# Mixture of experts: a second branch per expert behind the first product, and the gather and combine placed between the products

## The chip, the cores and the metric

The kernel runs on one core of one Trainium2 chip. The metric is device time in microseconds of the core, the median of three runs. One execution is also taken by the hardware profiler; its span is shown in the profile.

## The reference

The whole model is one dense block pair (a hybrid mixer and a SwiGLU, twice), and then a second block with two kinds of attention and a mixture of experts. The change touches only the mixture of experts, for 256 tokens of width 1024, 32 experts, four of them for each token:

```python
def clamped_swiglu(hdn):
    x_glu = jnp.minimum(hdn[..., :D_EXPERT], 7.0)
    x_lin = jnp.clip(hdn[..., D_EXPERT:], -7.0, 7.0)
    return x_glu * jax.nn.sigmoid(1.702 * x_glu) * (x_lin + 1)

logits = xt @ w_router + b_router
top_v, top_i = lax.top_k(logits, 4)
gates = jax.nn.softmax(top_v, axis=-1)
# for each expert e, over the tokens that chose it:
y = clamped_swiglu(x_e @ w_gate_up[e] + b_gate_up[e]) @ w_down[e] + b_down[e]
# out[token] += gate * y
x = x + gt_f * rms_norm(out, g_post_ffn)
```

`w_gate_up[e]` is 1024 x 2048 and `w_down[e]` 1024 x 1024, in float32: 12 MiB of weights for each expert, 384 MiB in all, each read once.

## The kernel before

The dense part takes the first 830 us or so and is not touched. The expert loop starts at line 1421 and is written out for 32 experts. A framework takes the program as written, tracks which instruction reads or writes which tile, and orders the instructions of each engine by readiness and by their place in the program; an instruction block under `tc.If` is placed as one unit on the engines that take part.

*Weights.* An expert's weights are 12 tiles of 1 MiB: eight of `w_gate_up` (`ws`, 128 rows each), four of `w_down` (`wd`). They go through a ring of 18 buffers (`RING2`, `etile`, line 1150). Only SyncE (SP) issues these loads, in order. At the head of expert e the loop asks for six tiles of expert e+1 (`nw.load(NEXT)`, line 1430), behind the branch of expert e for the other six (`nw.rest()`, line 1477). Tile i of the ring can be loaded when the 18th tile before it has been read for the last time.

*One expert.* Each expert has 64 places for tokens in the usual case. `g1` (line 1208) is the first product: 64 rows by 2048 columns over eight chunks of the depth, eight matmul instructions each in the trace, 64 in all, two column groups of the array at a time. The first two chunks and the bias (`begin`, line 1378) are asked for at the end of the expert before. `act` (line 1222) is the clamped SwiGLU: VectorE (DVE), ScalarE (ACT), DVE three times. `g2` (line 1234) turns the result with four transposes, copies it (line 1241), and makes the second product in 32 matmul instructions; ACT and DVE then split the result in a high and a low part (`yh`, `yl`, lines 1249 and 1250).

*A pair of experts.* Two experts share one gather and one combine. In an odd expert `pick_up` (line 1368) gathers the tokens of the next two with 32 one-hot matmuls, `places` turns the one-hot matrices for the combine (line 1257), `slot_gates` (line 1267) picks the gates. In an even expert `combine` (line 1286) adds the pair before to `acc`: eight matmuls (line 1284), in four PSUM banks, and four additions on DVE (line 1292). In expert 16 the bias of the second product is added for all experts. In the text "even" and "odd" are the number of the expert, counted from 0.

*The branch.* An expert with more than 64 tokens needs further places. `tc.If(n > 64)` at line 1463 stands behind `g2`; inside it `further(64)` gathers 32 more tokens (`extra_xt`), multiplies them with the same `ws` (`extra_in`) and `wd` (`extra_out`), and a nested `tc.If(n > 96)` (line 1470) does so again. PE, ACT and DVE take part. The number `n` is read into registers of the three engines (line 1436) from a one-element tile that POOL copies (line 1435). With these inputs experts 1 and 14 enter the outer branch, none the inner one. `many()` (line 1386) has one more branch, after expert 29, for over 128 tokens; it isn't entered.

*PSUM.* In this loop there are four banks for the first product (tag `g1`) and four for all the rest (`ps`).

*Residual.* `h`, 256 x 1024 in SBUF, holds the residual rows until the last additions (line 1490).

Of the kernel before, what the change touches and what calls it, by code (L numbers as in the profile page):

```python
# [20 lines left out]
P = 128  # L21
# [11 lines left out]

RING2 = (-1, 0, 1, -1, 2, 3, 4, 5, 6, 7, -1, -1, 8, 9, 10, 11, 12, 13)
EARLY = 10

MANY = 30

NEXT = len(RING2) - KC - KC // 2

# [58 lines left out]
def kernel_body(ctx, tc, I, out, stop=None, dbg=None):  # L99
# [20 lines left out]
    def wtile():  # L120
        return ring.tile([P, 2048], F32, tag="w", name=nm("w"))
# [4 lines left out]

    h = cpool.tile([P, 2, D], F32, name="h")
    nc.sync.dma_start(h[:, 0, :], I["x"][0:P, :])
# [659 lines left out]
    with ExitStack() as cx:  # L788
# [361 lines left out]
        def etile():  # L1150
            i = RING2[turn[0] % len(RING2)]
            turn[0] += 1
            if i < 0:
                return wtile()
            return (ring2 if i < 8 else ring3).tile([P, 2048], F32, tag=f"w{i}", name=nm("w2"))

        class Expert:

            def __init__(self, up, down, split=False):
                self.up, self.down, self.ws, self.wd, self.split = up, down, [], [], split  # L1160

            def load(self, n):
                for _ in range(n):
                    r = etile()
                    if len(self.ws) < KC:
                        nc.sync.dma_start(r, self.up(len(self.ws)))
                        self.ws.append(r)
                    else:
                        k = len(self.wd)
                        if self.split and k == KC // 2 - 1:  # L1170
                            for i in range(2):
                                nc.sync.dma_start(r[:, i * D:(i + 1) * D], self.down(k).rearrange("(p k) f -> p k f", k=2)[:, i])
                        else:
                            nc.sync.dma_start(r.rearrange("p (k f) -> p k f", k=2), self.down(k).rearrange("(p k) f -> p k f", k=2))
                        self.wd.append(r)
# [14 lines left out]
    with ExitStack() as cx:  # L1190

        mo = cx.enter_context(tc.tile_pool(name="mo", bufs=2, reuse_waits="tile"))

        bb = mo.tile([P, 2, 512], F32R, name="bb", bufs=1)
# [13 lines left out]
        def g1(banks, xt, ws, kcs):  # L1208

            for kc in kcs:  # L1210
                for b in range(2):
                    for a in range(2):
                        c0 = b * D + a * 512
                        TE.matmul(banks[b][64 * a:64 * a + 64, :], lhsT=xt[:, kc, :], rhs=ws[kc][:, c0:c0 + 512], start=kc == 0, stop=kc == KC - 1)  # L1214
# [100 lines left out]
        def extra_in(a, xt, sel, ws):  # L1315

            banks = [ps()[:, :256] for _ in range(2)]
            for b in range(2):
                for i in range(4):
                    TE.matmul(banks[b][32 * i:32 * i + 32, :], lhsT=sel(i // 2).to_broadcast([P, 32]),  # L1320
                              rhs=bb[:, b, 256 * (i % 2):256 * (i % 2) + 256].bitcast(F32), start=True, stop=False)
            for kc in range(KC):
                for b in range(2):
                    for i in range(4):
                        c0 = b * D + 256 * i
                        TE.matmul(banks[b][32 * i:32 * i + 32, :], lhsT=xt[:, kc, :], rhs=ws[kc][:, c0:c0 + 256], start=False, stop=kc == KC - 1)
            act(a[:, :256], banks)

# [11 lines left out]
        def extra_out(a, slot0, pm, gt, wd):  # L1340
            a, pg = a[:, :256], a[:, 256:].rearrange("p (a b) -> p a b", a=2)
            for t in range(2):
# [18 lines left out]
        def gathered(banks):  # L1361

            xt = mo.tile([P, KC, P], F32, tag="xt", name=nm("xt"), bufs=1)
            for i, q in enumerate(banks):
                (V.tensor_copy if i % 2 else S.copy)(xt[:, 4 * i:4 * i + 4, :].rearrange("p a b -> p (a b)"), q)
            return xt
# [19 lines left out]
        def many():  # L1386
# [4 lines left out]
            with tc.If(most > P):  # L1391
# [3 lines left out]
                with tc.For_i(0, NE, 1) as ei:  # L1395
# [3 lines left out]
                    for c in range(4):  # L1399
                        a1 = mo2.tile([P, 512], F32, tag="g", name=nm("og"), bufs=1)  # L1400
                        extra_in(a1, extra_xt(32 * c, lambda t: now[:, t, 0:1]), lambda q: now[:, 4 + q, 0:1], w.ws)
                        extra_out(a1, 32 * c, lambda t: now[:, t, 0:1], lambda t: now[:, 2 + t, 0:1], w.wd)
# [10 lines left out]
        nxt = begin(0, first)  # L1413
        ahead = places(), slot_gates(0)
        for t in range(2):
            S.copy(xmh[:, t, :], xm[:, t, :])
            V.tensor_sub(xml[:, t, :], xm[:, t, :], xmh[:, t, :].bitcast(F32))
        acc = xpool.tile([P, 2, D], F32, tag="xh", name="acc")
        G.memset(acc, 0.0)
        y = last = None  # L1420
        for e in range(NE):
# [14 lines left out]
            n = nc.values_load(ne[0:1, 0:1], engines=[mybir.EngineType.PE, mybir.EngineType.Activation, mybir.EngineType.DVE],  # L1436
                               min_val=0, max_val=T)
            if e + 1 == NE:
                gp2 = mo.tile([P, D], F32, tag="xt", name="gp2", bufs=1)
                nc.scalar.dma_start(gp2, lastd[0].partition_broadcast(P))  # L1440
            elif j:
                xt = pick_up()
                ahead = places(), slot_gates(e + 1)
            if j == 0:
                if last is not None:
                    combine(*last)
                if e == NE // 2:

                    g4, bd = [mo.tile([P, 2, 512], F32, tag=tag, name=nm(tag), bufs=1) for tag in ("yh", "yl")]
                    g4, bd = g4[:, :, :P], bd[:, 0, :256]  # L1450
                    gT = mo2.tile([P, T], F32, tag="oT", name="gT", bufs=1)
                    nc.scalar.dma_start(bd, I["b_down"])
                    for t in range(2):
                        G.tensor_copy(g4[:, t, :].rearrange("p (a b) -> p a b", a=4), copies4(gate[:, t, :]))
                    turned(gT, g4)
                    combine4(gT, bd)
                y = [mo.tile([P, 2, 512], F32R, tag=tag, name=nm(tag), bufs=1) for tag in ("yh", "yl")]
            if e + 1 == NE:
                fin = [[psum.tile([P, 512], F32, tag="g1", name=nm("fin")) for _ in range(2)] for _ in range(2)]
                carry(fin)  # L1460
            g2(a, w.wd, y, j)
            pm, gt = (lambda t: posm[:, t, e:e + 1]), (lambda t: gate[:, t, e:e + 1])
            with tc.If(n > 64):  # L1463
                def further(slot0):
                    o = mo2.tile([P, 512], F32, tag="g", name=nm("og"), bufs=1)
                    extra_in(o, extra_xt(slot0, pm), lambda q: qe[:, q, e:e + 1], w.ws)
                    extra_out(o, slot0, pm, gt, w.wd)

                further(64)
                with tc.If(n > 96):  # L1470
                    further(96)
                if e + 1 == NE:
                    carry(fin, True)
            if e + 1 == MANY:
                many()
            if e + 1 < NE:
                nw.rest()
                nxt = begin(e + 1, nw)
# [9 lines left out]
        for t in range(2):  # L1488
            for a, b, o in zip(halves(acc[:, t, :]), halves(h[:, t, :]), halves(out[t * P:(t + 1) * P, :])):
                V.scalar_tensor_tensor(b, a, r[t][:, 0:1], b, ALU.mult, ALU.add)  # L1490
                nc.sync.dma_start(o, b)
# [42 lines left out]
```

## Time and profile before

| | |
|---|---|
| median of three runs | 1964.48 us (1957.91 to 1967.62) |
| the profiled execution | 1965.33 us, its span 1963.6 us |
| PE busy | 1774.7 us, 90% of the span |
| DVE, ACT, POOL busy | 783.2, 522.4, 164.5 us |
| DMA | 568.48 MB, mean 290 GB/s |
| mean granted clock of PE | 0.957 |

PE is the matmul engine, PEld its weight loads, which overlap with matmuls. A name with a q (PEq, PEldq, SPq) is the engine's sequencer, where waits, branches and the issue of DMAs stand; these do not count as busy time. Ends of matmuls are modelled. L1463 is line 1463 of the kernel before. Times in a timeline are microseconds from the start of the span.

### The profile page before, as it was taken

How to read it: one execution, taken by the hardware profiler on the slowest of the kernel's cores; microseconds unless marked ns; L12 is line 12 of the kernel's file. 1: busy time of each engine (PE TensorE's matmuls, PEld its weight loads, DVE VectorE, ACT ScalarE, POOL GpSimd, SP SyncE). 2: the span in 40 equal slices, each digit the busy share in tenths (PEclk: the TensorE clock that was granted, in tenths of full speed). 3: DMA queues.
4: the chain of work that ended last, by engine and by line, in shares of the span. 5: the costliest groups of instructions: out<-in, count | busy, mean ns of one | idle time of the engine just before them, and what ended most of it. 6: DMA issues, size and time to landing. Idle time of an engine off the chain costs nothing. (4 is left out here: it accounts for less than half of the span.)

```text
span 1963.6 us, 23687 instructions
## 1 busy us (share of the span) xinstructions
PE 1774.7 (90%) x9432; PEld 1083.8 (55%) x9432; DVE 783.2 (40%) x1267; ACT 522.4 (27%) x892; POOL 164.5 (8%) x261
## 2 busy tenths in 40 slices
PE   8999999999999999988888898988888989898986
PEld 6888997787899788734333332334333333233322
DVE  5677775667777667522112112211212111211122
ACT  5645444565444455311000101010001010101011
POOL 1131210113111130010000000000000000000000
PEclk9999999999999999888999999999899999999998
DMA  9537786433788673816999899996789999999976
GB/s 303 147 118 236 246 278 228 152 129 114 249 260 277 211 257 129 352 50 249 398 372 379 358 413 379 379 380 252 287 348 373 378 417 383 380 378 407 393 289 254
DMA packets 160403, 568.48 MB, mean 290 GB/s; under 512 B 15426, under 2 KB 66124, under 8 KB 111060
## 3 DMA queue, kind: packets, MB, share of 16 engines
q1 hardware_dynamic: 149560, 552.42, 72.9%
q10 hardware_dynamic: 9852, 11.57, 1.8%
q0 software_dynamic: 800, 1.77, 0.8%
q8 instruction: 141, 2.31, 0.5%
q14 instruction: 50, 0.41, 0.1%
HBM read 563.06 MB, written 2.66 MB: 288 GB/s over the span
## 5 line engine op out<-in xcount | busy, mean ns | idle before, releaser
L1214 PE MATMUL g<-w,xt 128*64 128x512 f32 x2048 | 518.6, 609 | 31.5 <-PEq L1463 17.6
L1214 PEld LDWEIGHTS g<-w,xt 128*64 128x64 f32 x2048 | 147.5, 138 | 303.8 <-issue 292.3
L251 DVE TENSOR_TENSOR wlo<-w,whi 128x1024 fp32r<-128x1024 f32 x203 | 256.4, 1268 | 100.7 <-ACT whi L250 96.7
L1247 PE MATMUL ps<-w,aT 128*64 128x512 f32 x1024 | 264.1, 674 | 22.6 <-ACT aT L1241 22.6
L250 ACT CAST whi<-w 128x1024 fp32r<-128x1024 f32 x203 | 211.2, 1045 | 180.0 <-PE ps L257 87.2
L256 PE MATMUL ps<-xh,whi 128*128 128x256 f32 x792 | 227.9, 288 | 0.0
L257 PE MATMUL ps<-xh,wlo 128*128 128x256 f32 x792 | 223.3, 282 | 0.0
L258 PE MATMUL ps<-xl,whi 128*128 128x256 f32 x792 | 223.2, 282 | 0.0
L1247 PEld LDWEIGHTS ps<-w,aT 128*64 128x64 f32 x1024 | 80.2, 155 | 186.7 <-issue 155.0
L1250 DVE TENSOR_TENSOR yl<-ps,yh 64x512 fp32r<-64x512 f32 x64 | 44.1, 689 | 339.4 <-ACT yh L1249 338.4
L256 PEld LDWEIGHTS ps<-xh,whi 128*128 128x128 f32 x792 | 149.5, 189 | 2.1 <-PE ps L405 1.0
L257 PEld LDWEIGHTS ps<-xh,wlo 128*128 128x128 f32 x792 | 149.4, 189 | 2.1 <-issue 1.7
L258 PEld LDWEIGHTS ps<-xl,whi 128*128 128x128 f32 x792 | 149.4, 189 | 0.0
L1226 ACT ACTIVATE g<-g 128x512 f32<-128x512 f32 x32 | 19.2, 601 | 347.8 <-DVE g L1225 347.8
L1249 ACT CAST yh<-ps 64x512 fp32r<-64x512 f32 x64 | 37.1, 579 | 267.4 <-PE ps L1247 266.6
L1111 DVE TENSOR_SCALAR pos<-idio,posm 128x64 fp32r<-128x64 f32 x64 | 12.9, 251 | 221.7 <-PE ps L1267 221.6
L1225 DVE TENSOR_SCALAR g<-g 128x512 f32<-128x512 f32 x32 | 22.1, 692 | 181.3 <-PE g L1214 181.3
L1239 PE MATMUL ps<-idio,g 128*128 128x128 f32 x128 | 26.6, 339 | 71.1 <-DVE g L1232 71.1
L1218 POOL CAST pick<-qe 128x128 fp32r<-128x128 f32 x32 | 9.4, 293 | 953.9 <-PE g L1220 953.6
L256 PE MATMUL ps<-whi,xh 128*128 128x512 f32 x176 | 72.5, 412 | 2.1 <-ACT xh L214 1.3
L1258 ACT CAST pT<-ps 128x256 fp32r<-128x256 f32 x16 | 6.0, 372 | 254.4 <-PE ps L1257 247.9
L1239 PEld LDWEIGHTS ps<-idio,g 128*128 128x128 f32 x128 | 19.3, 211 | 96.7 <-issue 50.9
(372 smaller groups left out, 2527.3 us busy)
## 6 DMA issues: line engine op xcount, KB each, us to landing
w<-in_w_gate_up_dram SPq DMA_DIRECT2D x256, 1024.0 KB, 18.0
w<-in_w_down_dram SPq DMA_DIRECT2D x149, 1024.0 KB, 10.6
w<-in_w_in_dram SPq DMA_DIRECT2D x32, 1024.0 KB, 6.8
w<-in_w_ada_dram SPq DMA_DIRECT2D x24, 1024.0 KB, 5.3
w<-in_w_gate_dram SPq DMA_DIRECT2D x22, 1024.0 KB, 8.1
w<-in_w_up_dram SPq DMA_DIRECT2D x22, 1024.0 KB, 5.4
w<-in_w_out_dram SPq DMA_DIRECT2D x12, 1024.0 KB, 5.1
w<-in_w_in_dram SPq DMA_DIRECT2D x8, 512.0 KB, 9.0
```

The source lines that it names most:

```text
L250: S.copy(hv, self.raw)
L251: V.tensor_sub(lv, self.raw, hv.bitcast(F32))
L256: TE.matmul(o, lhsT=ah, rhs=bh, start=first, stop=False)
L257: TE.matmul(o, lhsT=al, rhs=bh, start=False, stop=False)
L258: order[TE] = TE.matmul(o, lhsT=ah, rhs=bl, start=False, stop=last)
L1214: TE.matmul(banks[b][64 * a:64 * a + 64, :], lhsT=xt[:, kc, :], rhs=ws[kc][:, c0:c0 + 512], start=kc == 0, stop=kc == KC - 1)
L1225: V.tensor_scalar(out=a, in0=gl, scalar1=7.0, scalar2=None, op0=ALU.min)
L1226: S.activation(gl, a, AF.Sigmoid, scale=1.702)
L1239: TE.transpose(q[:, i * P:(i + 1) * P], av[:, i // 2, i % 2, :], ident)
L1247: TE.matmul(q[at[b], :], lhsT=aT[:, f % 4, 64 * (f // 4):64 * (f // 4) + 64], rhs=wd[f // 2][:, c0:c0 + 512], start=f == 0, stop=f == KC - 1)
L1249: S.copy(y[0][at[b], b, :], q[at[b], :])
L1250: V.tensor_tensor(out=y[1][at[b], b, :], in0=q[at[b], :], in1=y[0][at[b], b, :].bitcast(F32), op=ALU.subtract)
```

## The change

The branch behind the second product is split in two. The first, behind the first product, does `extra_in` for the further places (all that reads `ws`); the second, behind the second product, does `extra_out` (all that reads `wd`). The result between them is kept in two tiles `og`. All 12 loads of the next expert are asked for behind the first product, except for the expert before `many()`. `pick_up`, `places`, `slot_gates` and `combine` are queued on PE behind the last matmul of the first product (`issue_after` sets the order of issue on that engine, without a wait). The count of an expert is copied on POOL behind the copy of the bias pick of that expert. The rows of `h` are written to DRAM ahead of the loop, its buffer takes the place of the 18th ring buffer, and the rows are read back in the last expert. The split of the tokens in `xmh` and `xml` is queued behind the copies of the first gather.

```diff
+HOME = 99
+RING2 = (-1, 0, 1, -1, 2, 3, 4, 5, 6, 7, -1, -1, 8, 9, 10, 11, 12, HOME)
-NEXT = len(RING2) - KC - KC // 2
...
+homed = dram.tile([2, P, D], F32, name="homed")
...
+            if i == HOME:
+                return cpool.tile([P, 2048], F32, tag="h", name=nm("w2"))
...
+        for t in range(2):
+            nc.scalar.dma_start(homed[t], h[:, t, :])
...
-            G.tensor_copy(pick, qe[:, :, e:e + 1].to_broadcast([P, 2, 64]))
+            order[G] = G.tensor_copy(pick, qe[:, :, e:e + 1].to_broadcast([P, 2, 64]))
...
-        ahead = places(), slot_gates(0)
-        for t in range(2):
-            S.copy(xmh[:, t, :], xm[:, t, :])
-            V.tensor_sub(xml[:, t, :], xm[:, t, :], xmh[:, t, :].bitcast(F32))
+        with tc.issue_after(order[TE].ins):
+            ahead = places(), slot_gates(0)
+        with tc.issue_after(order["up"][0].ins), tc.issue_after(order["up"][1].ins):
+            for t in range(2):
+                S.copy(xmh[:, t, :], xm[:, t, :])
+                V.tensor_sub(xml[:, t, :], xm[:, t, :], xmh[:, t, :].bitcast(F32))
...
+            g1(banks, xe, w.ws, range(AHEAD, KC))
+            through = order[TE].ins
+            ne = spool.tile([1, 1], I32, tag="ne", name=nm("ne"), bufs=2)
+            with tc.issue_after(order[G].ins):
+                G.tensor_copy(ne, cnt[0:1, e:e + 1])
+            n = nc.values_load(ne[0:1, 0:1], engines=ARMS, min_val=0, max_val=T)
             if e + 1 < NE:
                 nw = expert(e + 1)
-                nw.load(NEXT)
-            g1(banks, xe, w.ws, range(AHEAD, KC))
+                nw.load(len(RING2) - KC - KC // 2 if e + 1 == MANY else KC + KC // 2)
             a = mo2.tile([P, 512], F32, tag="g", name=nm("g"), bufs=1)
             act(a, banks, gs[:, j:j + 1])
-            ne = spool.tile([1, 1], I32, tag="ne", name=nm("ne"), bufs=2)
-            G.tensor_copy(ne, cnt[0:1, e:e + 1])
-            n = nc.values_load(...)
+            more = [mo2.tile([P, 256], F32, tag="og", name=nm("og"), bufs=2) for _ in range(2)]
+            with tc.If(n > 64):
+                extra_in(more[0], extra_xt(64, pm), sel, w.ws)
+                with tc.If(n > 96):
+                    extra_in(more[1], extra_xt(96, pm), sel, w.ws)
...
+                home = etile().rearrange("p (t d) -> p t d", t=2)
+                for t in range(2):
+                    nc.sync.dma_start(home[:, t, :], homed[t])
-            elif j:
-                xt = pick_up()
-                ahead = places(), slot_gates(e + 1)
-            if j == 0:
-                if last is not None:
-                    combine(*last)
+            with tc.issue_after(through):
+                if j and e + 1 < NE:
+                    xt = pick_up()
+                    ahead = places(), slot_gates(e + 1)
+                if j == 0:
+                    if last is not None:
+                        combine(*last)
...
             g2(a, w.wd, y, j)
             with tc.If(n > 64):
-                def further(slot0):
-                    o = mo2.tile([P, 512], F32, tag="g", name=nm("og"), bufs=1)
-                    extra_in(o, extra_xt(slot0, pm), lambda q: qe[:, q, e:e + 1], w.ws)
-                    extra_out(o, slot0, pm, gt, w.wd)
-
-                further(64)
+                extra_out(more[0], 64, pm, gt, w.wd)
                 with tc.If(n > 96):
-                    further(96)
+                    extra_out(more[1], 96, pm, gt, w.wd)
...
             if e + 1 == MANY:
                 many()
+                nw.rest()
             if e + 1 < NE:
-                nw.rest()
                 nxt = begin(e + 1, nw)
```

## Rows read from the trace of the kernel before

**Rows 1.** Busy time by stage: stretch, length, five engines, granted clock, DMA share, GB/s.

```profile
835.00:875.60 40.60, 35.15 (x139) 15.15 (x140) 9.33 (x17) 6.00 (x11) 5.40 (x14) 0.86 0.01 2
875.60:926.80 51.20, 42.94 (x377) 22.63 (x374) 11.72 (x31) 5.76 (x14) 0.53 (x3) 0.95 0.61 248
...
957.50:1346.40 388.90, 340.80 (x1484) 129.80 (x1483) 76.44 (x144) 37.94 (x78) 3.53 (x12) 0.95 0.93 382
1346.40:1380.90 34.50, 26.93 (x284) 15.56 (x280) 6.71 (x18) 2.94 (x7) 0.00 (x0) 0.87 0.25 102
```

**Rows 2.** Waits of SP's queue, from 850 us: us in total, times, longest.

```profile
SPq L1166 <- PEq L1463: 505.7, 28, 55.3
```

**Rows 3.** Busy time by stretch, one odd and one even expert, columns as before.

```profile
1222.80:1253.00 30.20, 26.67 (x120) 11.37 (x122) 4.84 (x13) 2.82 (x7) 0.29 (x1) 0.89 1.01 419
1222.80:1258.20 35.40, 31.74 (x140) 12.77 (x141) 5.18 (x14) 3.75 (x9) 0.29 (x1) 0.90 0.92 382
1258.20:1287.80 29.60, 25.62 (x110) 9.11 (x111) 7.57 (x12) 2.58 (x5) 0.29 (x1) 1.00 0.97 397
...
1245.75:1252.58 6.83, 5.93 (x16) 2.21 (x18) 0.02 (x1) 0.58 (x1) 0.00 (x0) 0.50 1.02 422
```

**Rows 4.** Timeline of PE, even expert: start, length, instruction, [idle before <- releaser].

```profile
1264.64 10.52 PE L1214 MATMUL g<-w,xt 128*64 128x512 f32 x48
1277.33 0.75 PE L1239 MATMUL ps<-idio,g 128*128 128x128 f32 x4 [2.17 <-DVE g L1232]
1278.81 7.09 PE L1247 MATMUL ps<-w,aT 128*64 128x512 f32 x32 [0.73 <-ACT aT L1241]
...
1287.82 1.47 PE L1214 MATMUL g<-w,xt 128*64 128x512 f32 x5 [1.07 <-PEq L1463]
```

**Rows 5.** Timeline of PE, odd expert.

```profile
1228.55 1.94 PE L1214 MATMUL g<-w,xt 128*64 128x512 f32 x8
...
1230.58 0.27 PE L1374 MATMUL ps<-pos,xmh 128*128 128x128 f32 x1
1230.69 0.28 PE L1374 MATMUL ps<-pos,xml 128*128 128x128 f32 x1
...
1231.23 1.94 PE L1214 MATMUL g<-w,xt 128*64 128x512 f32 x8
...
1239.09 0.51 PE L1267 MATMUL ps<-gate,pos 128*128 128x2 f32 x4
...
1245.92 1.10 PE L1239 MATMUL ps<-idio,g 128*128 128x128 f32 x4 [2.74 <-DVE g L1232]
1247.75 9.46 PE L1247 MATMUL ps<-w,aT 128*64 128x512 f32 x32 [0.73 <-ACT aT L1241]
...
1258.22 1.90 PE L1214 MATMUL g<-w,xt 128*64 128x512 f32 x6 [0.15 <-PEq L1463]
```

**Rows 6.** Branch lines: ns min/median/max, first and last start; experts 12, 11, 14, 14.

```profile
L1463 PEldq COMPARE_BRANCH  x1: 6185/6185/6185, 1281.5 to 1281.5; - x1
...
L1463 PEldq COMPARE_BRANCH  x1: 4434/4434/4434, 1252.8 to 1252.8; - x1
...
L1463 PEldq COMPARE_BRANCH  x1: 82/82/82, 1346.4 to 1346.4; - x1
...
L1470 PEldq COMPARE_BRANCH  x2: 193/1848/3504, 1376.9 to 1380.7; - x2
```

**Rows 7.** The line of the combine's additions: ns min/median/max.

```profile
L1292 DVE TENSOR_TENSOR acc<-acc,ps x60: 679/686/689, 930.1 to 1898.9; 128x512 f32<-128x512 f32 x60
```

**Rows 8.** Waits between 835 and 850 us: us in total, times, longest.

```profile
PE g L1220 <- POOL ne L1435: 5.2, 1, 5.2
```

**Rows 9.** Timeline of PE, expert 0.

```profile
848.21 16.42 PE L1214 MATMUL g<-w,xt 128*64 128x512 f32 x64
```

**Rows 10.** Waits of PE from 926.8 us to the end.

```profile
PE g L1214 <- PEq L1463: 17.6, 21, 5.1
...
PE ps L1334 <- ACTq L1470: 0.5, 1, 0.5
```

More of the change, by code (lines that the diff above doesn't have):

```diff
@@ L124, in small @@
         return spool.tile([P, n], dtype, tag=tag, name=nm(tag), bufs=bufs)
-    h = cpool.tile([P, 2, D], F32, name="h")
+    h = cpool.tile([P, 2, D], F32, tag="h", name="h")
     nc.sync.dma_start(h[:, 0, :], I["x"][0:P, :])
@@ L1154, in etile, with __init__ @@
                 return wtile()
+            if i == HOME:
+                return cpool.tile([P, 2048], F32, tag="h", name=nm("w2"))
             return (ring2 if i < 8 else ring3).tile([P, 2048], F32, tag=f"w{i}", name=nm("w2"))
         class Expert:
-            def __init__(self, up, down, split=False):
-                self.up, self.down, self.ws, self.wd, self.split = up, down, [], [], split
+            def __init__(self, up, down, split=False, queue=nc.sync):
+                self.up, self.down, self.ws, self.wd, self.split, self.queue = up, down, [], [], split, queue
             def load(self, n):
@@ L1165, in load @@
                     if len(self.ws) < KC:
-                        nc.sync.dma_start(r, self.up(len(self.ws)))
+                        self.queue.dma_start(r, self.up(len(self.ws)))
                         self.ws.append(r)
@@ L1326, in extra_in @@
                         TE.matmul(banks[b][32 * i:32 * i + 32, :], lhsT=xt[:, kc, :], rhs=ws[kc][:, c0:c0 + 256], start=False, stop=kc == KC - 1)
-            act(a[:, :256], banks)
+            act(a, banks)
         def combine4(pT, y):
@@ L1340, in extra_out @@
         def extra_out(a, slot0, pm, gt, wd):
-            a, pg = a[:, :256], a[:, 256:].rearrange("p (a b) -> p a b", a=2)
+            pg = mo2.tile([P, 512], F32, tag="g", name=nm("opg"), bufs=1)[:, :256].rearrange("p (a b) -> p a b", a=2)
             for t in range(2):
@@ L1364, in gathered @@
             for i, q in enumerate(banks):
-                (V.tensor_copy if i % 2 else S.copy)(xt[:, 4 * i:4 * i + 4, :].rearrange("p a b -> p (a b)"), q)
+                order.setdefault("up", []).append((V.tensor_copy if i % 2 else S.copy)(xt[:, 4 * i:4 * i + 4, :].rearrange("p a b -> p (a b)"), q))
             return xt
@@ L1399, in many @@
                     for c in range(4):
-                        a1 = mo2.tile([P, 512], F32, tag="g", name=nm("og"), bufs=1)
+                        a1 = mo2.tile([P, 256], F32, tag="og", name=nm("og"), bufs=2)
                         extra_in(a1, extra_xt(32 * c, lambda t: now[:, t, 0:1]), lambda q: now[:, 4 + q, 0:1], w.ws)
@@ L1440, in kernel_body @@
                 nc.scalar.dma_start(gp2, lastd[0].partition_broadcast(P))
-            elif j:
-                xt = pick_up()
-                ahead = places(), slot_gates(e + 1)
-            if j == 0:
-                if last is not None:
-                    combine(*last)
[L1447 to L1457, printed above, removed]
@@ L1458, in kernel_body @@
-            if e + 1 == NE:
-                fin = [[psum.tile([P, 512], F32, tag="g1", name=nm("fin")) for _ in range(2)] for _ in range(2)]
-                carry(fin)
+                home = etile().rearrange("p (t d) -> p t d", t=2)
[8 more added lines that the diff above has]
+                        combine(*last)
+                    if e == NE // 2:
+                        g4, bd = [mo.tile([P, 2, 512], F32, tag=tag, name=nm(tag), bufs=1) for tag in ("yh", "yl")]
+                        g4, bd = g4[:, :, :P], bd[:, 0, :256]
+                        gT = mo2.tile([P, T], F32, tag="oT", name="gT", bufs=1)
+                        nc.scalar.dma_start(bd, I["b_down"])
+                        for t in range(2):
+                            G.tensor_copy(g4[:, t, :].rearrange("p (a b) -> p a b", a=4), copies4(gate[:, t, :]))
+                        turned(gT, g4)
+                        combine4(gT, bd)
+                    y = [mo.tile([P, 2, 512], F32R, tag=tag, name=nm(tag), bufs=1) for tag in ("yh", "yl")]
+                if e + 1 == NE:
+                    fin = [[psum.tile([P, 512], F32, tag="g1", name=nm("fin")) for _ in range(2)] for _ in range(2)]
+                    carry(fin)
@@ L1488, in kernel_body @@
         for t in range(2):
-            for a, b, o in zip(halves(acc[:, t, :]), halves(h[:, t, :]), halves(out[t * P:(t + 1) * P, :])):
+            for a, b, o in zip(halves(acc[:, t, :]), halves(home[:, t, :]), halves(out[t * P:(t + 1) * P, :])):
                 V.scalar_tensor_tensor(b, a, r[t][:, 0:1], b, ALU.mult, ALU.add)
```

13 lines of the change are left out of this document (6 added, 7 removed).

## The prediction

> **What bounds the kernel now.** I read the page first: TensorE (PE) is busy nine tenths of the span. The next view is the busy time by stage: in a long undisturbed stretch of the expert loop the DMA engines stand at 0.93 as well, around expert 1 at 0.61, at expert 14 at 0.25 [rows 1]. Two engines near full, and neither quite, call for the third view. In the waits of the DMA-issuing queue SP stood 505.7 us, 28 times, for PE's sequencer to pass line 1463, the branch on more than 64 tokens [rows 2]. The weight buffers are read inside that branch, so they come free only when PE is through it; at that moment all 12 buffers that SP wants are free together.
>
> The fourth view cuts one pair of experts at that branch. An odd expert takes 35.4 us, an even one 29.6, 65.0 the pair, 32.5 each [rows 3]. In the odd one the DMA share is 1.01 over the first 30.2 us, and 0.92 over all 35.4, so 0.40 over the last 5.2: the 12 transfers are through before PE reaches the branch. Transfers alone would need 30.0 to 30.2 us an expert, so PE's chain from branch to branch sets the pace, by 2.4 us. What I predict is therefore the length of that chain, with the transfers as a floor.
>
> The fifth and sixth views are PE's own timeline. Even expert [rows 4]: 48 matmuls of the first product in 10.52 us (0.219 each); 2.17 us idle for the activation chain; transposes; 0.73 idle for a copy; the second product; 1.07 us idle at the branch. Odd expert [rows 5]: between groups of eight first-product matmuls lie some six of the gather, 0.11 us apart, at 2.68 us a round; the idle is 2.74, and then the second product takes 9.46 us in place of 7.09. There the granted clock is 0.50, the lower of its two levels (1.2 of 2.4 GHz) [rows 3], and PE had been idle just before.
>
> **The chain in parts.** First product: 62 matmuls after the branch by 0.219 is 13.6, bias 0.6, one change of shape 0.2: 14.4. Transposes to second product (1277.33 to 1278.81): 1.5. Second product to the next start behind the branch (1278.81 to 1287.82): 9.0. Base 24.9 us, in both kinds. An even expert adds 2.17 idle and 2.5 for eight combine matmuls with the changes of shape around them: 29.6. An odd one adds 2.74, 32 gather matmuls (3.6), the turned one-hots and slot gates (about 0.65; the gates' row alone has 0.51), 2.7 of slow clock, some 1.7 of changes of shape, less 0.9 because its branch shows 0.15 and not 1.07: 35.4. Both agree with the stretches [rows 3].
>
> **The change, part by part.** *Gather and combine tied behind the first product.* They leave the first product and come to the place where PE is idle now. The changes of shape go (1.7 in odd experts, about 0.7 in even). Only what is longer than the idle time is still paid.
>
> *The first branch behind the first product.* A branch that is entered takes 82 ns [rows 6]; one that is jumped takes 6.185 us in an even expert, with transfers at 0.97, and 4.434 in an odd one, where they had ended. The sequencer runs ahead of the array: it begins the branch at 1281.5, with two thirds of the second product still to run (it began at 1278.81 and takes 7.09), which hides all but 1.07 us of the 6.2. Transfers will now run beside nearly every branch, so I take 6.2 for all. Bounds for what stays bare at the new branch: nothing (the matmuls behind it hide it) and 6.2 (nothing is queued). I take 1.07, since the same kind of matmuls stands before it, 62 in a row.
>
> The Trainium skill says of this ("Runtime: NRT & Kernel Launch", Instruction fetch mechanics) that a taken branch whose target lies outside the window of loaded instructions forces a DMA fetch before execution goes on. The trace agrees: the entered branch is short, the jumped one long. That rule speaks against the change, which doubles such fetches; what it would make of the time is the third rival.
>
> So an even expert: 1.07, then eight combine matmuls by 0.235 (1.9), and 0.3 because these hold the PSUM banks until VectorE has added them (0.686 each [rows 7], behind its activation chain): 3.3 in place of 4.7. That is 28.2 us, 1.4 less. An odd expert: 1.07, gather 3.6, one-hots and gates 0.65, a change of shape and the copies 0.4: 5.7, while the activation chain runs beside it. The gap that came before the slow clock is then filled. That is 24.9 + 5.7 = 30.6, 4.8 less. If a gap stays, the 2.7 us are lost again.
>
> *Buffers free earlier, all 12 loads asked for at once.* SP's queue does nothing but loads here; what it is moved past is only the first product. After the first branch eight buffers are free, after the second four. PE at a mean of 29.4 us would just be under the transfers' 30.0, but transfers start earlier around expert 1: now they stand at 0.01 from 835 to 876, with 18 buffers full [rows 1]. Eight buffers would be free at about 860. I count 30 transfers done at about 898 (branch 1 entered, its buffers held until then), and PE at the end of expert 1 at about 920: a lead of 8 transfers, 20 us, and 0.6 of it is used up in an expert. Expert 14, with 34.5 us between its branch and the next start [rows 1], gives it back. So earlier transfers are worth little by themselves.
>
> *Counts one expert ahead.* Now POOL copies counts ahead of the first bias pick: PE waits 5.2 us for it [rows 8], and the 64 matmuls behind it take 16.42 us, 2.4 more than at 0.219 each [rows 9]. Later each engine reads one count per expert, ahead of need; I cost that at nothing (it hides behind queued matmuls as the branch does; bare it would be 0.3 to 0.5). Start: 7.6 less.
>
> *Residual rows to DRAM and back.* Two 512 KB writes go out where DMA is idle (share 0.01), two reads on SP behind the last expert's weights, needed only by the very last additions, while the last second product runs. Nothing; uncovered some 2 to 5 us once. The buffer it frees only replaces another in the ring, so the depth stays 18.
>
> *Two entered branches.* Experts 1 and 14 now pass the nested jump (line 1470) twice: 3.5 us with nothing queued [rows 6]. Plus 3.5 each, less 1.7 of shape changes in expert 1.
>
> **Sum.** Start −7.6; expert 1 +1.8; experts 2 to 30, 15 even by −1.4 is −21, 14 odd (31 has no gather) by −4.8 is −67.2; expert 14 +3.5: −90.5. On the profiled execution's span of 1963.6: 1873.1; with the 1.7 us outside the span (1965.33) 1874.8. The median of the runs shown, 1964.48, lies 0.9 below that execution, so nothing is corrected. **1875 us.**
>
> **The rivals.** *The branch is not where PE's idle time is.* The program puts the activation chain ahead of the first branch. If VectorE and ScalarE meet the branch after it, the PSUM banks used inside are given back only then, and gather and combine must wait for it: PE waited for ScalarE's passing of a branch at 1470 already [rows 10]. Then the idle 2.2 stays, followed by the moved work: even 29.9, odd 31.7, 30.8 on average, 1.4 worse than forecast, 1917. With the slow clock in every pair (2.7) 1958. For it: banks are four, and the branch uses six. Against it: gather may be issued ahead of the branch.
>
> *The transfers become the bound.* If the new branch stays fully hidden and the copies cost nothing, PE needs 28.4: 1845, and less if expert 14's delay is made good out of the 18 buffers. The floor is 354 transfers by 2.5 us from 898, 1783, and 15 to 20 for the rest: about 1800.
>
> *The first branch stands bare.* If only a few matmuls are queued when the sequencer reaches it (a last weight tile that lands late, a wait for a bank ahead of the branch), 6.2 us and not 1.07 go onto 31 experts: +5.1 each, about 2030. This decides from 2.9 us more per expert on, where the 90 us are eaten: when over 4.0 of the 6.2 us are bare. For it: at expert 30, where PE waited for a transfer first, the same branch cost 5.1 [rows 10]. Against it: elsewhere 1.07 or 0.15.
>
> *No change.* Half of each: moved work after the idle, slow clock, 1.5 us bare. About 1965.
>
> **Chances and numbers.** Forecast (1850 to 1897) 0.45; transfers or perfect filling (1800 to 1850) 0.13; waits for the branch (1897 to 1955) 0.24; no change 0.06; bare branch, slower, 0.12. Half a per cent, 10 us, is about what a measurement of this kernel can tell from no change (its runs spread 1957.91 to 1967.62): faster 0.82, same 0.06, slower 0.12. The range takes in the second rival and the upper part of the first: 1830 to 1955.
>
> **What would show it.** Right: PE's idle behind the first product (now 2.17 and 2.74) shrinks to about one; second products all near 7.1 us; odd experts near 30.6; SP's wait is split over two branches; jumped branches all near 6 us. Wrong: the idle stays and the gather follows it (first rival), or PE stands 4 to 6 us at the new branch (third).

## The result, and the profile after

The changed kernel takes 1902.79 us (median of four runs, 1898.46 to 1907.79); the kernel before took 1966.05 in the same session. The ratio is 0.969, with an interval of 0.965 to 0.973: faster by 3.1%, where 4.6% was forecast. The time lies in the range given (1830 to 1955), 28 us above the forecast. Of the classes with chances it lies in "waits for the branch" (1897 to 1955, 0.24), 6 us outside the forecast's own (1850 to 1897, 0.45). The profiled execution has a span of 1899.3 us, 26.2 above the 1873.1 forecast for it.

The timeline of PE for one pair, an odd expert and then an even one (start, length, instruction, [idle before <- releaser]; some lines are left out, above all the 32 gather matmuls of the odd expert and seven combine matmuls of the even one):

```profile
1198.69 3.62 PE L1218 MATMUL g<-w,xt 128*64 128x512 f32 x14 [1.48 <-PEq L1484]
1202.24 0.73 PE L1227 MATMUL g<-bb,pick 128*128 128x512 f32 x2
1204.25 8.80 PE L1218 MATMUL g<-w,xt 128*64 128x512 f32 x40 [1.28 <-POOL ne L1441]
1214.98 1.94 PE L1218 MATMUL g<-w,xt 128*64 128x512 f32 x8 [1.92 <-PEq L1452]
...
1220.71 0.51 PE L1274 MATMUL ps<-gate,pos 128*128 128x2 f32 x4
1221.08 0.70 PE L1246 MATMUL ps<-idio,g 128*128 128x128 f32 x4
1222.52 7.09 PE L1254 MATMUL ps<-w,aT 128*64 128x512 f32 x32 [0.73 <-ACT aT L1248]
...
1234.81 8.80 PE L1218 MATMUL g<-w,xt 128*64 128x512 f32 x40
1245.35 1.94 PE L1218 MATMUL g<-w,xt 128*64 128x512 f32 x8 [1.74 <-PEq L1452]
1247.22 0.50 PE L1291 MATMUL ps<-yh,pT 128*128 128x512 f32 x1
...
1249.93 0.75 PE L1246 MATMUL ps<-idio,g 128*128 128x128 f32 x4 [0.59 <-DVE g L1239]
1251.41 7.09 PE L1254 MATMUL ps<-w,aT 128*64 128x512 f32 x32 [0.74 <-ACT aT L1248]
```

Read against [rows 4, 5]: the first product runs in one piece, gather and combine follow it, the transposes start right behind the gather (the idle of 2.74 us is gone) and 0.59 us behind the combine (2.17 before). Both second products take 7.09 us; the 9.46 at half clock is gone. Two waits are new, both in the first product: 1.28 us for POOL's copy of a count, and 1.74 to 1.92 us at the first branch, L1452. The same two stretches by busy time (length, five engines, granted clock, DMA share, GB/s), beside [rows 3]:

```profile
1198.69:1231.47 32.78, 28.69 (x145) 12.46 (x145) 6.11 (x14) 3.98 (x9) 0.41 (x2) 1.00 0.99 393
1231.47:1259.50 28.03, 24.82 (x106) 8.96 (x107) 5.57 (x10) 2.13 (x4) 0.41 (x2) 1.00 1.01 416
```

The even expert is as forecast (28.0 against 28.2). The odd one is 2.2 us too long (32.8 against 30.6). In this pair transfers run all the time. PE's waits from 880 us to the end (us in total, times, longest):

```profile
PE g L1218 <- PEq L1452: 45.7, 26, 2.5
PE ps L1254 <- ACT aT L1248: 22.4, 30, 1.0
PE g L1218 <- POOL ne L1441: 15.7, 12, 1.6
PE g L1218 <- PEq L1484: 14.4, 20, 1.5
PE g L1218 <- DMA w<-in_w_gate_up_dram: 6.3, 3, 2.5
PE ps L1246 <- DVE g L1239: 5.4, 9, 0.6
```

The idle of the activation chain, 71.1 us in 29 waits before, is down to 5.4 in 9. The first branch and the count stand in its place with 61.4; the second branch has 14.4, where the one branch before had 17.6 in 21. The two branches on PE's sequencer (ns min/median/max, first and last start):

```profile
L1452 PEldq COMPARE_BRANCH  x34: 70/6047/6249, 837.7 to 1867.2; - x34
...
L1484 PEldq COMPARE_BRANCH  x32: 70/2912/6630, 865.0 to 1882.8; - x32
```

The next table sets the forecast beside all kernels run, by stretches from the start of one second product on PE to another (expert 3 to 13 are five ordinary pairs, 17 to 29 six; expert 14 enters its branches; `many()` stands at expert 30). Each row is one profiled execution, in us.

| kernel | to 3 | 3 to 13 | 13 to 17 | 17 to 29 | 29 to 31 | rest | span |
|---|---|---|---|---|---|---|---|
| before | 983.9 | 328.8 | 169.4 | 390.2 | 72.3 | 19.0 | 1963.6 |
| forecast | 971.9 | 297.8 | 160.5 | 353.0 | 70.9 | 19.0 | 1873.1 |
| after | 971.8 | 311.9 | 152.3 | 376.8 | 67.3 | 19.2 | 1899.3 |
| x1_tie_only | 973.2 | 304.2 | 157.8 | 363.9 | 75.1 | 18.9 | 1893.1 |
| x2_untied | 976.9 | 313.1 | 153.0 | 373.8 | 69.8 | 19.2 | 1905.8 |
| x3_early_counts | 975.0 | 318.3 | 151.3 | 372.0 | 70.0 | 19.2 | 1905.8 |
| x4_tie_start | 967.2 | 302.9 | 157.9 | 363.9 | 67.9 | 18.9 | 1878.7 |
| y1_inside | 973.3 | 336.3 | 158.5 | 408.6 | 74.8 | 19.2 | 1970.7 |
| y2_one_branch | 966.7 | 301.7 | 160.4 | 366.2 | 74.9 | 19.2 | 1889.1 |
| y3_late_branch | 974.1 | 332.4 | 166.7 | 389.0 | 70.1 | 19.2 | 1951.4 |
| y4_less_pe | 968.8 | 308.4 | 149.5 | 368.9 | 71.2 | 19.2 | 1885.9 |
| z1_start_only | 978.0 | 329.3 | 169.8 | 390.5 | 72.4 | 19.0 | 1959.0 |
| z2_tie_start_home | 971.6 | 302.8 | 158.4 | 364.1 | 74.8 | 19.2 | 1890.9 |
| z3_tie_start_bias | 969.6 | 302.5 | 151.5 | 366.5 | 67.9 | 18.9 | 1876.9 |
| w1_rows_by_pool | 978.3 | 317.5 | 160.9 | 375.3 | 68.0 | 18.8 | 1918.9 |

The 26 us come from the ordinary pairs, which are 14.1 and 23.8 too long: 3.4 us for each of the eleven (62.6 on the mean, 59.2 forecast). The stretches of experts 14 and 30 gave 8.2 and 3.6 back. The pair in the timeline, 60.8, is a short one: it is cut behind a wait of 1.48 us at the second branch, and no stall falls in it. A pair with a stall, from expert 19 to 21, takes 66.6.

### The profile page after: what moved, and what is told of

Its sections match the earlier page's. It is cut to its first block, busy times and chain, and to the rows that moved or that the text cites. A ratio compares the mean times of both kernels' runs of the same rounds, so it can differ in the third digit from the quotient of the medians.

```text
span 1899.3 us, 23884 instructions
## 1 busy us (share of the span) xinstructions
PE 1723.6 (91%) x9432; PEld 1085.1 (57%) x9432; DVE 781.4 (41%) x1267; ACT 522.5 (28%) x892; POOL 161.4 (8%) x261
## 5 line engine op out<-in xcount | busy, mean ns | idle before, releaser
L1218 PE MATMUL g<-w,xt 128*64 128x512 f32 x2048 | 508.1, 611 | 89.3 <-PEq L1452 45.7
L1218 PEld LDWEIGHTS g<-w,xt 128*64 128x64 f32 x2048 | 162.5, 139 | 405.9 <-issue 358.6
L1254 PE MATMUL ps<-w,aT 128*64 128x512 f32 x1024 | 231.2, 602 | 22.4 <-ACT aT L1248 22.4
L1254 PEld LDWEIGHTS ps<-w,aT 128*64 128x64 f32 x1024 | 74.0, 139 | 158.1 <-issue 125.8
L256 PE MATMUL ps<-whi,xh 128*128 128x512 f32 x176 | 72.4, 411 | 1.9 <-ACT xh L214 1.0
L257 PE MATMUL ps<-whi,xl 128*128 128x512 f32 x176 | 71.0, 403 | 1.5 <-DVE xl L215 1.5
L258 PE MATMUL ps<-wlo,xh 128*128 128x512 f32 x176 | 70.2, 399 | 0.0
L491 DVE SCALAR_TENSOR_TENSOR modm<-w,cond,modm 128x512 f32<-128x512 f32 x84 | 65.0, 773 | 7.6 <-DMA w<-in_w_ada_dram 5.9
L748 POOL TENSOR_TENSOR al<-sg,ah 128x256 fp32r<-128x256 f32 x36 | 44.9, 1247 | 209.1 <-ACT ah L747 209.1
```

What stands on the lines that cost most here:

```text
L256: TE.matmul(o, lhsT=ah, rhs=bh, start=first, stop=False)
L257: TE.matmul(o, lhsT=al, rhs=bh, start=False, stop=False)
L258: order[TE] = TE.matmul(o, lhsT=ah, rhs=bl, start=False, stop=last)
L491: V.scalar_tensor_tensor(m, w, c, m, ALU.mult, ALU.add)
L748: G.tensor_tensor(out=al[:, f, :], in0=a, in1=ah[:, f, :].bitcast(F32), op=ALU.subtract)
L1218: order[TE] = TE.matmul(banks[b][64 * a:64 * a + 64, :], lhsT=xt[:, kc, :], rhs=ws[kc][:, c0:c0 + 512], start=kc == 0, stop=kc == KC - 1)
```

## The experiments

My theory after the result: the gain is the move of gather and combine out of the first product and into PE's idle time; the second branch earns nothing for it (theory A in the expectations of the first kernels). The rival (theory B): the eight buffers that come free one product earlier are what pays. Times below are medians, with the ratio to the kernel before and its interval.

**Is it the move?** Three kernels.

`x1_tie_only`: the kernel before with the move alone. One branch, at its old place; residual rows, counts and loads as before.

```diff
+            through = order[TE].ins      # last matmul of the first product
...
+            with tc.issue_after(through):
                 (pick_up, places, slot_gates, combine)
```

> The kernel before, with one part of the change: gather and combine queued behind the last matmul of the first product. One branch, counts, loads and residual as before. Theory A (the gain is PE's chain: work moved into idle time, changes of shape and the slow clock saved): even experts 27.4 us and odd ones 29.5, under the 30.0 that 12 transfers take, so 30.0 to 30.3 an expert and about 1892 to 1900 us in all, with the second product at 7.1 us in odd experts too. Theory B (the gain is the buffers that come free earlier): buffers come free as before, so 1955 to 1965 us.

1894.86 us, ratio 0.966 (0.963 to 0.969). The move alone gives the whole gain, with the buffers coming free as late as before.

`x2_untied`: the changed kernel without `issue_after(through)`.

> The changed kernel without the tie: gather and combine may again be issued inside the first product. Two branches, counts and loads as changed. Theory A: all that the tie saved is lost and the second branch stays, so 33 us an expert or more, 1965 to 1990 us. Theory B: the buffers still come free behind the first product, so the gain stays, 1900 to 1915 us.

1905.48 us, 0.970 (0.969 to 0.972). The number is theory B's, but the kernel doesn't tell the two apart: in its timeline of PE, gather and combine still stand behind the first branch and behind the last eight matmuls of the first product. They stay there without the tie, so the move wasn't undone.

`y1_inside`: the move undone. Gather and combine are written ahead of the first branch, untied; both branches, early buffers, counts and rows stay. With this the branch also comes to stand behind gather and combine, as in `y3_late_branch` below.

```diff
-            with tc.If(n > 64):          # first branch
-                extra_in(...)
-            with tc.issue_after(through):
-                (pick_up, places, slot_gates, combine)
+            (pick_up, places, slot_gates, combine)
+            with tc.If(n > 64):
+                extra_in(...)
```

> The changed kernel with gather and combine written ahead of the first branch and not tied, so that PE has them among the first product's matmuls again, as before the change; both branches, the early buffers and the counts stay. Theory A (the gain is the move into the gap; the second branch costs some 1.8 us an expert): the changes of shape, the idle of 2.2 to 2.7 and the slow second products are back, and the branch is on top: 1955 to 1995. Theory B (the eight buffers that come free a product earlier are worth most of the gain): at most 1920.

1974.30 us, 1.006 (1.004 to 1.009): a little slower than the kernel before. Its timeline of PE, here an even expert, has the old idle back, with the branch on top:

```profile
1268.40 1.94 PE L1218 MATMUL g<-w,xt 128*64 128x512 f32 x8 [1.82 <-PEq L1479]
1272.59 0.81 PE L1246 MATMUL ps<-idio,g 128*128 128x128 f32 x4 [2.25 <-DVE g L1239]
1274.13 9.94 PE L1254 MATMUL ps<-w,aT 128*64 128x512 f32 x32 [0.73 <-ACT aT L1248]
```

That second product by busy time (columns as above):

```profile
1274.13:1283.90 9.77, 9.77 (x32) 2.98 (x33) 0.00 (x0) 0.00 (x0) 0.00 (x0) 0.70 1.01 420
```

The granted clock is 0.70, so part of it ran at the lower of the two levels (1.2 and 2.4 GHz), behind 1.82 and 2.25 us of idle; in the kernel before, 2.17 us alone left the second product of an even expert at 7.09 us.

Not all of the 72 us over the changed kernel are the move's. `y3_late_branch` keeps the tie, has the branch behind gather and combine too, and takes 1952.68 us. What `y1_inside` shows is that early buffers bring no gain here over the branch that they need; what they are worth without its cost, no run shows. The rival falls by the kernels with one branch: `x1_tie_only` here, and `x4_tie_start` and `y2_one_branch` below, have the whole gain and no buffer earlier.

**What do the other parts cost or bring?**

`y2_one_branch`: the changed kernel with both bodies in one branch behind the second product.

> The changed kernel with both bodies in one branch behind the second product; the tie, the counts, the order of the loads and the residual rows in DRAM stay as in the changed kernel. Theory A (the first branch, bare by 1.76 us, and its count read ahead of it are pure cost): 1872 to 1885, odd experts near 31, no idle behind a count. Theory B (the split earns what it costs, and the counts or the residual rows are what costs): 1898 to 1910.

1894.70 us, 0.964 (0.961 to 0.968): between the theories. Here theory A is that the first branch and the count read ahead of it are pure cost, theory B that the split earns what it costs. The medians of this and the changed kernel lie 8 us apart and their intervals overlap, but the stretches are clear: without the first branch the eleven pairs take 60.7 us each and not 62.6 (667.9 and 688.7 over eleven), while experts 13 to 17 take 160.4 and not 152.3. So the split costs 1.9 us in a pair and earns 8 around expert 14; 7.4 of these are there by the second product of expert 15. At expert 1, the other that enters its branches, it earns 1.1: from expert 0 to 3 the changed kernel takes 112.3 us and this one 113.4. At expert 14 the `ws` tiles are released ahead of `extra_out`, and SP gets its next eight loads out 38.19 us after the first of them, in place of 55.51 (the changed kernel, then this one):

```profile
1279.59 38.19 SPq L1168 DMA_DIRECT2D w<-in_w_gate_up_dram  x8
```

```profile
1281.32 55.51 SPq L1168 DMA_DIRECT2D w<-in_w_gate_up_dram  x8
```

`x3_early_counts`: the changed kernel, all counts copied behind the first bias pick.

```diff
-            order[G] = G.tensor_copy(pick, ...)
+            order.setdefault(G, G.tensor_copy(pick, ...))
```

> The changed kernel, with all counts copied behind the first bias pick alone, so that PE reads them at the head of the loop and not in each expert. Theory A1 (the read behind the bias holds PE's sequencer until POOL has copied, and takes away the matmuls that should hide the first branch): the 1.28 us in odd experts go and the first branch shows 0.8 to 1.1 us instead of 1.76, together 25 to 40 us, 1865 to 1880 us. Rival A2 (the read hides behind queued matmuls, the branch is bare for its own length): 1895 to 1905 us.

1910.93 us, 0.974 (0.972 to 0.977): both missed; the median is 8 us above the changed kernel's, and the intervals just touch. The wait for POOL is gone from the list (one of 4.5 us is left at the start, ahead of the stretch listed), but PE's at the first branch grew and a wait for nothing that the profile shows came up:

```profile
PE g L1218 <- PEq L1453: 50.5, 27, 4.0
PE ps L1255 <- ACT aT L1249: 21.9, 29, 1.0
PE g L1218 <- issue: 10.4, 5, 4.6
```

Where nothing disturbs, the step does what was expected: from expert 6 to 10 this kernel takes 120.8 us, 60.4 a pair, and the changed kernel 124.0. It loses that elsewhere: 105.7 us and not 94.5 from expert 10 to 13, where three such waits of 1.2 to 2.4 us fall and some second products are at a lowered clock again (9.9 us at expert 11, and at 29). Why these waits come, stays open.

`x4_tie_start`: `x1_tie_only`, and all counts copied behind the first pick.

> The kernel before with the tie, and with the counts copied behind the first bias pick alone. One branch. Theory A: as the run with the tie alone, less 7 to 8 us at the start, 1884 to 1893 us, faster than the changed kernel although no buffer comes free earlier. Theory B: 1948 to 1958 us.

1879.67 us, 0.957 (0.954 to 0.959): below the changed kernel's interval, and 15 us below x1, where 8 were expected.

`z1_start_only`: the counts behind the first pick, on the kernel before and by itself.

> The kernel before, with all counts copied behind the first bias pick and nothing else. By the forecast's term for the start: 7.6 us less, 1954 to 1960. By the difference between the two earlier kernels that have the tie, without and with this step (1894.9 and 1879.7): 15 us less, 1945 to 1952, with half of it inside the loop and not at the start.

1960.12 us, 0.997 (0.996 to 0.999), by this ratio 5.5 us less (2.2 to 8.6). The term of 7.6 lies inside; the 15 don't. By the table 6.0 of the 15 are at the start and 7.2 at experts 29 to 31, where x1 has a stall that x4 lacks (PE's timeline, x1 and then x4):

```profile
1814.33 4.94 PE L1214 MATMUL g<-w,xt 128*64 128x512 f32 x10 [6.41 <-issue]
```

```profile
1801.76 2.76 PE L1214 MATMUL g<-w,xt 128*64 128x512 f32 x10 [1.07 <-PEq L1466]
```

"Issue" means that PE waited for nothing the profile shows. In x1 the instruction queue's next packet went out at 1811.95 us, when PE was dry already; in x4 the corresponding packet, at 1804.92, came while matmuls ran. So I take the stall for a wait for instructions, which is argued and not shown. The packet itself is not later: it goes out 12.8 us behind the start of expert 29's second product in x1, 13.0 in x4. Why PE needs it earlier in one kernel than in the other wasn't settled.

`z2_tie_start_home`: x4 and the residual rows in DRAM.

```diff
+            nc.scalar.dma_start(homed[t], h[:, t, :])       # ahead of the loop
...
+                    nc.sync.dma_start(home[:, t, :], homed[t])   # last expert
```

> The kernel with the tie and the counts behind the first pick (1879.7), plus the residual rows in DRAM and back. By the forecast (the rows cost nothing, hidden beside PE's work at both ends): 1874 to 1885, ratio to the kernel before as without them, 0.954 to 0.960. Rival: the rows are what holds the one-branch form of the change at 1894.7: 1890 to 1898.

1892.93 us, 0.963 (0.961 to 0.966): 13 us more than x4, so the rival's number. The table puts 4.4 of the 12.2 us of the profiled spans at the start and 6.9 at experts 29 to 31 (the stall again, 6.7). The rest of the kernel, the tail included, is the same to 0.9. At the start SP waits for the write of the rows (its waits from 796 to 832 us):

```profile
SPq L1208 <- DMA homed<-h: 12.5, 1, 12.5
SPq L1170 <- DMA homed<-h: 9.1, 1, 9.1
```

And in PE's timeline the first bias comes late, with 64 matmuls at a lowered clock behind it (13.95 us in x4):

```profile
841.84 0.70 PE L1226 MATMUL g<-bb,pick 128*128 128x512 f32 x2 [2.77 <-DVE gs L1277]
842.47 15.65 PE L1220 MATMUL g<-w,xt 128*64 128x512 f32 x64
```

`w1_rows_by_pool`: the changed kernel, these two writes issued by POOL, to take that wait off SP.

```diff
-            nc.scalar.dma_start(homed[t], h[:, t, :])
+            nc.gpsimd.dma_start(homed[t], h[:, t, :])
```

> The changed kernel with the two writes of the residual rows issued by POOL instead of ScalarE, so that they take another set of the framework's DMA semaphores and SP's loads no longer wait for them (12.0 and 9.3 us before the second load of the bias table and the next weight tile). If that wait is what the rows cost: the bias table is there by 818, PE does not stand 3.1 us at the first bias, the first product of expert 0 is at full clock, expert 0's second product begins near 854 and not at 859.5: 1894 to 1899. Rival (the write itself, its traffic or the later code, is the price, not the wait): 1900 to 1906.

1909.72 us, 0.972 (0.970 to 0.974). The edit took away only one of SP's two waits for the rows: the second bias load goes out at 805.7 and not 814.7 us, but the next weight tile still waits:

```profile
SPq L1168 <- DMA homed<-h: 10.8, 1, 10.8
```

PE stands 3.68 us at the first bias all the same. The two copies of the table run on ScalarE and VectorE at 844.69 and 845.77 us there, 39 us behind that load's issue and right behind the copies of the gates (in x4 at 830.22 and 832.46). That points to the order of the work on these engines and not to the load. My cause for the rows' price falls, and with it I can't say that the rows cost anything by themselves: y2 has them too and starts as early as x4 (966.7 and 967.2).

**Where could the first branch stand?** `y3_late_branch`: the changed kernel with the first branch behind gather and combine.

> The changed kernel with the first branch behind gather and combine on PE, no longer between the first product's last matmuls. Theory A (the branch stands bare by 1.76 us because only the sequencer's run-ahead of 4 to 5 us hides it; behind the gather it falls together with the idle of the activation chain): odd experts lose 2 to 3 us, even ones under 1, until transfers stop it: 1868 to 1885. Theory B (the 6 us only move and now hold up the transposes; all that waits for the branch on ScalarE and VectorE comes later too): 1900 to 1925.

1952.68 us, 0.994 (0.992 to 0.996): slower than both theories said. PE's waits:

```profile
PE ps L1246 <- DVEq L1479: 35.7, 15, 2.5
PE ps L1246 <- PEq L1479: 27.1, 10, 3.9
```

One odd expert in PE's timeline:

```profile
1600.37 1.10 PE L1246 MATMUL ps<-idio,g 128*128 128x128 f32 x4 [1.87 <-DVEq L1479]
1602.20 9.07 PE L1254 MATMUL ps<-w,aT 128*64 128x512 f32 x32 [0.73 <-ACT aT L1248]
```

Here the transposes wait for VectorE's passing of the branch, 1.9 to 2.5 us, and nearly every second product is at a lowered clock (8.4 to 9.8 us). This is the first rival of the prediction, the branch on the wrong side of the activation chain. It was priced at 1917, or 1958 with the slow clock in every pair.

**What stops it?** `y4_less_pe`: the changed kernel without the low parts in gather and combine. Half of those matmuls are left out.

> The changed kernel without the low parts in gather and combine (their matmuls are left out: 16 of 32 in an odd expert, 1.8 us, and 4 of 8 in an even one, 0.9 us); all transfers stay. Theory A (PE's chain sets the pace of the changed kernel, transfers do not): about 41 us less, 1855 to 1870. Theory B (transfers at 30.0 to 30.3 us an expert are the bound already): at most 15 us less, 1887 to 1900.

1898.06 us, 0.966 (0.963 to 0.970): theory B's number (transfers are the bound already), but not its proof. Of the 41 us of work, part had been lying in the idle of the activation chain (PE's wait for DVE's `g` grew from 5.4 to 19.7 us), and the wait for the count came to even experts too (15.7 to 27.1). The DMA share went from 0.97 to 1.00 between experts 17 and 29. The test mixes three limits and proves none.

`z3_tie_start_bias`: x4 with `b_down` asked for at the head of expert 16.

> The kernel with the tie and the counts behind the first pick (1879.7), with the bias of the second product for all experts asked for at the head of expert 16 and not in the middle of it. PE stood 7.2 us for it there, and its second product took 9.2 us in place of 7.1: if PE's chain decides there, as after the stall of the transfers at expert 14, 6 to 9 us less, 1870 to 1875. If the transfers make up for it (they had a lead), no change, 1877 to 1883.

1874.28 us, 0.954 (0.952 to 0.957), the best measured: 1.5% under the changed kernel, their intervals apart. Against x4 the intervals overlap. Experts 13 to 17 took 6.4 us less, and 2.6 came back in the pairs behind them.

## Why the prediction was right, and 28 us too good

The range was 125 us wide, wider than the gain forecast, and the total came out nearer than its parts: the pairs missed by 38 us, and 12 came back elsewhere. Of these, 8.2 have the sign opposite to their term, and the 3.6 at expert 30 lie within what comes and goes there without an edit's doing (see the last section); that much of the hit is luck.

**The move: right in its mechanism and its place.** Changes of shape, idle and half clock went as forecast, and the even expert came out at 28.0 us; x1 shows that this alone carries the change.

**The first branch: the step that was mis-sized.** I took 1.07 us bare (not covered by matmuls); it was 45.7/26 = 1.76. The step said that the same kind of matmuls stands before the new branch, 62 in a row. On PE the branch came ahead of the last eight of them, and what covers it is not their number but how far the sequencer runs ahead of the array. At the old place the branch began at 1281.5, and the array ran dry at 1286.75 us (two matmuls of the next product stood there as well): 5.25 us of cover. At the new place it began at 1239.2, and the forty matmuls ended at 1243.61: 4.4 us.

```profile
L1452 PEldq COMPARE_BRANCH  x1: 5932/5932/5932, 1239.2 to 1239.2; - x1
```

Over 26 experts the difference of 0.69 is 18 us. "Jumped branches all near 6 us" holds for the first branch (median 6.05), not for the second (2.91), which stood bare for 14.4 us in all.

**The counts: costed at nothing, 15.7 us.** I hid the read behind queued matmuls, as the branch. In odd experts the read stands on PE right behind the bias, and POOL's copy of the next count right behind its next pick, which itself must wait for that bias. Nothing is queued, so PE stands 1.28 us. In the even expert shown, matmuls stand between, and it is free. These two steps together are 2.1 us in an odd expert, which is the 2.2 it is too long. They don't simply add: without the first branch (y2) a pair takes 60.7 us though 17.2 us of waits for the count are left, and without the count (x3, where nothing disturbs) 60.4. Either brings the pair down to the floor below.

**The transfers: a floor I let the forecast pass under.** The forecast pair was 59.2 us on the mean of the eleven. With the move and with one branch (x4) the pairs take 60.6, in both stretches:

```profile
967.20:1270.10 302.90, 271.46 (x1252) 107.73 (x1252) 63.49 (x122) 31.73 (x66) 2.97 (x10) 0.97 1.01 414
1428.00:1791.90 363.90, 325.90 (x1502) 129.60 (x1502) 75.53 (x141) 38.02 (x79) 3.55 (x12) 0.98 1.01 416
```

The DMA share is 1.01 there: 24 MiB (25.17 MB) by 416 GB/s is 60.5 us. So 1.4 of the 3.4 us that a pair missed were not to be had, even with both steps at my price; the other 2.0 go with the first branch (1.9 by y2). The changed kernel's own pairs, five and then six:

```profile
971.80:1283.70 311.90, 271.21 (x1250) 110.89 (x1250) 63.44 (x121) 31.60 (x66) 4.13 (x20) 0.99 1.00 409
1435.90:1812.70 376.80, 327.63 (x1500) 134.79 (x1500) 75.91 (x143) 37.95 (x79) 4.96 (x24) 0.98 0.97 398
```

In the six the transfers plainly had idle time; in the five they stood at 1.00 as well, moving 409 GB/s and not 414, so there PE and the transfers are both near their limit. The second rival was that bound, with a branch that hides; I gave it 0.13 and let the lead of eight transfers carry the forecast past it.

**Expert 14: the other sign.** I added 3.5 us for two nested jumps; the stretch came out 8.2 under the forecast; y2, which has no first branch, took 160.4 against the 160.5 forecast, so the split with its earlier release is what earns it. **Early buffers elsewhere: worth little**, as said: x4 beats the changed kernel without them, and what they would be worth without the branch no run shows. **Start: right** (z1 within its interval). **Residual rows: open**, as told above.

**The third rival** took place in part: 1.76 of 6 us bare, far from the 4.0 at which it would have decided. The first branch takes 6.05 us (median) when it is jumped beside transfers, and 0.07 when it is entered; the instruction queue carried 178 packets, where the kernel before had 141. The Trainium skill says ("Runtime: NRT & Kernel Launch", Instruction fetch mechanics) that a jump out of the loaded instructions has to wait for a fetch by DMA; the trace agrees.

## What to carry to other kernels

Put matmuls that depend on nothing in it into the idle time behind a chain of other engines: up to the length of that idle they cost nothing, and here the granted clock of what followed stayed up (7.09 us in place of 9.46). A branch on TensorE costs what its sequencer's run-ahead doesn't cover, so look up when it starts and when the array runs dry, at the very place where it will stand, and look at where the other engines pass it. Where a second engine stands at 0.93, work out its floor for the very unit in which the gain is counted, before the gains are summed.

## What was not expected of the hardware

A transfer bound can hide in a branch's name. In x4 PE's list of waits from 880 us on has hardly any for weights, while transfers set the pace:

```profile
PE g L1214 <- PEq L1466: 53.8, 27, 5.4
...
PE g L1214 <- DMA w<-in_w_gate_up_dram: 3.7, 4, 2.2
```

Behind expert 6 PE stood 4.60 us at the branch; the weight tile that the matmul ahead of the branch reads had been asked for at 1038.37 and landed 20.5 us later, at 1058.92, and the sequencer began the branch at 1058.96, with 1.5 us of work left in the array (the rest of the second product and two matmuls; they ended at 1060.50). Elsewhere it had up to 5.3 us; the run-ahead was used up in the wait for the tile. Up to expert 13 the other waits of over 1.3 us at this branch look the same, with a tile landed 0.04 to 0.06 us ahead of it; from expert 17 on no landing on record lies that close, and there the reading is not shown. PE's timeline:

```profile
1059.48 1.02 PE L1214 MATMUL g<-w,xt 128*64 128x512 f32 x2
1065.10 3.64 PE L1214 MATMUL g<-w,xt 128*64 128x512 f32 x6 [4.60 <-PEq L1466]
```

The issue of that tile (count, KB, us to landing), in the view of the DMA queues:

```profile
w<-in_w_gate_up_dram SPq DMA_DIRECT2D x1, 1024.0 KB, 20.5
```

And the branch (columns as above):

```profile
L1466 PEldq COMPARE_BRANCH  x1: 5972/5972/5972, 1059.0 to 1059.0; - x1
```

Behind this stall the clock was down too: six matmuls took 3.64 us at a granted clock of 0.50, where fourteen take 3.62 in the changed kernel. And kernels whose edits have nothing to do with expert 30 differed there by 7 us, by the stall named "issue": below half a per cent, a difference between two kernels of this program need not be their edit's.
